# Matmul with rotary embedding on one core: two more block pairs, and stores in paced quarters

## The chip, the core and the metric

The kernel runs on one core of a Trainium2 chip. The metric is the device time of the program in microseconds (us). Before the change the median of three runs is 149.89 us (149.50 to 150.14). The execution that was profiled took 149.84 us, of which 148.1 us is the span from the first to the last instruction.

## The reference

```python
# x (16, 512, 768), weight (768, 768), cos and sin (512, 64), all float32; n_heads = 12
y = np.matmul(x, weight).reshape(16, 512, 12, 64)
y1, y2 = y[..., :32], y[..., 32:]
out1 = y1 * cos1 - y2 * sin1      # cos1, sin1: first 32 columns, one row per position
out2 = y2 * cos2 + y1 * sin2      # cos2, sin2: last 32 columns
out = np.concatenate([out1, out2], axis=-1).reshape(16, 512, 768)
```

25.2 MB of x come in and 25.2 MB go out; between them are one matrix product with a fixed 768x768 weight and a rotation that needs two products and a sum per element.

## The kernel before

**Tiles and groups.** The 8192 rows of x are cut into 64 tiles of 128 rows. Partition p of a tile holds position 4p + r of one batch, so a tile has one r and one batch. Four tiles with one r are a group (`QB = 4`), there are 16 groups (`LAST = 15`), and a group's second half, its third and fourth tile, is "pair (g, 1)".

**Two ways in.** An ordinary tile is loaded whole by SyncE (`load`, 128 rows of 3072 B, into one of `NX = 10` buffers xs), cast to fp16 on ScalarE (`cast`, xc<-xs), transposed on TensorE in twelve 64-row pieces (`turn_rows`, L272, into PSUM tile pt) and copied back by ScalarE (xt<-pt). A pair named in `BLOCKS` comes in as a block pair: four quarter loads (`load_quarter`, L226, each into 32 partitions, 256 pieces of 768 B), then one 32x32 block transpose on VectorE (`turn_pair`, L300) in place of TensorE's work. A block pair marked "sp" is loaded by SyncE into one of `NB = 3` buffers xb and cast by one wide ScalarE cast (`cast_pair`, xd<-xb). One marked "pool" is loaded by GpSimd, with the cast in the DMA, into xh. Before the change the block pairs are the second halves of groups 4 to 13 and 15; of these 5, 7, 9, 11, 13 and 15 are "sp".

**The product.** `walk` and `one` (L362) issue the matmuls of a pair as two interleaved streams of 64-row halves into six PSUM banks, three for each pair. When the banks of a unit are complete, `rope` has VectorE multiply them by cos and by the signed sin (L443) into a buffer tq, or into the memory of the raw weight w_raw, which is one of the three homes used in turn. GpSimd adds the two products into the output buffer ov (L465). There are `NOV = 4` output buffers, one for each group in turn, so the add of group g + 4 waits until the stores of group g have landed. The last three groups use smaller units, and the last one also sums some of its units on VectorE and TensorE. `ident32`, an fp32 identity for a TensorE sum in the very last group, lies in the memory of w_raw and is written by GpSimd in the iteration of tile 8 (L718); VectorE's next product in that home waits for it.

**What sets the order.** All is written out by hand in one loop over the tiles i. Iteration i issues, in this order: the matmuls of tile i with one `turns` among them, `rope` as units become complete, `bturns` (block transposes about four tiles ahead), another `turns`, `casts` (about six tiles ahead), `pool_loads` (twenty tiles ahead), and the stores listed under i in the table `stores`. Each engine works through its own instructions in that order; `Flow.do` puts semaphore waits where data demand it, and `Flow.settle` leaves out waits that are already implied. SyncE's loads follow the list `fetch`; `pump` issues from it as far as free buffers allow, and the quarters of an "sp" pair are mixed with the tile loads that come before its turn.

**Stores.** Groups 0 to 12 are stored from ScalarE's queue, half a group at a time (two tiles, 768 KB, 256 pieces of 3072 B; L497). Groups 13 and 14 are stored by SyncE, and the last group by both in smaller pieces. A store waits for the GpSimd adds of its half. For groups 4 to 9 the two halves stand under tiles 4g + 10 and 4g + 12.

Of the kernel before, what the change touches and what calls it, by code (L numbers as in the profile page):

```python
# [10 lines left out]
FP32 = mybir.dt.float32  # L11
# [5 lines left out]
class Flow:  # L17
# [24 lines left out]
    def do(self, e, make, reads=(), writes=(), dma=None, tick=True, after=0):  # L42
        need = {}
        for k in reads:
            for s, v in self.wrote.get(k, {}).items():
                need[s] = max(need.get(s, 0), v)
        for k in writes:
            for d in (self.wrote, self.readby):
                for s, v in d.get(k, {}).items():
                    need[s] = max(need.get(s, 0), v)  # L50
        if e == "pe":
            need.pop("pe", None)
            if after:
                need["pe"] = after
        waits = self.settle(e, need)
        for s, v in waits[:-1]:
            self.eng[e].wait_ge(self.sem(s), v)  # L57
        i = make(self.eng[e])
        if waits:
            s, v = waits[-1]  # L60
            i.wait_op(self.sem(s), v, "sem-ge")
        name, step = (dma, 16) if dma else (e, 1)
        self.sem(name)
        self.order[name] = len(self.order) + sum(self.count.values())
        at = self.count[name] + step
        if tick or dma:
            i.then_inc(self.sems[name], step)
            self.count[name] = at
            self.known[name, at] = dict(self.seen[e])
        for k in reads:  # L70
            d = self.readby.setdefault(k, {})
            d[name] = max(d.get(name, 0), at)
        for k in writes:
            self.wrote[k] = {name: at}
            self.readby[k] = {}
        return i
# [32 lines left out]
def kernel(  # L109
# [10 lines left out]
    nc = tc.nc  # L120
    f = Flow(nc, tc)
    do = f.do
    P = nc.NUM_PARTITIONS

    B, S, H = x.shape
# [6 lines left out]
    SB = S // P  # L132
    QB = 4
# [3 lines left out]
    LAST = NG - 1  # L137


    BLOCKS = {}  # L140
    for g in range(5, 14):
        BLOCKS[g, 1] = "pool" if g % 2 == 0 and g >= 4 else "sp"
    BLOCKS[LAST, 1] = "sp"
    BLOCKS[4, 1] = "pool"

    def sbuf(name, shape, dt):
        return nc.alloc_sbuf_tensor(name, shape, dt).ap()
# [3 lines left out]
    ident = sbuf("ident", [P, P], FP16)  # L151
# [13 lines left out]
    w_flat = w_raw.rearrange("p t e n -> p (t e n)")  # L165
# [7 lines left out]
        v = mem[:, base : base + 2 * n].rearrange("p (j n) -> p j n", j=2)  # L173
        return v[:, :, lo:hi], sorted(keys)

    ident32 = w_flat[:, 3072 : 3072 + P]
    HOMES0, HOMES, HOMESL = (0, 1024, 3072, 4096), (6144, 0, 3072), (0, 1024, 2048, 3072, 4096, 5120)
    ov_b = [sbuf(f"ov{i}", [P, QB * H], FP32) for i in range(NOV)]
    py = nc.alloc_psum_tensor("py", [P, 6 * 512], FP32).ap()
# [14 lines left out]
    def where(i):  # L194
        g, s = divmod(i, QB)
        return QB * (g // SB) + s, g % SB

    def pair_of(i):
        return i // QB, (i % QB) // 2
# [31 lines left out]
    def load_w(c, e="sp"):  # L231
        t, h = c
        do(e, lambda eng: eng.dma_start(out=w_raw[:, t, h], in_=wv[t, h]),  # L233
           writes=[f"wr{t}{h}"], dma=f"ov{t}_0" if h else f"xb{t}")

    def cast_w(c, e):
        t, h = c
# [249 lines left out]
    def store(g, c0, c1, e):  # L487
# [11 lines left out]
           dma=f"xs{c0 // 256 % NX}" if (c1 - c0) % H else f"ov{o}_{c0}")  # L499


    do("dve", lambda eng: eng.memset(cold, 0.0), writes=["cold"])  # L502
    do("pool", lambda eng: eng.memset(ident, 0.0), writes=["ident"])
    do("pool", lambda eng: eng.affine_select(
        out=ident, in_=ident, compare_op=mybir.AluOpType.not_equal, fill=1.0,
        base=0, pattern=[[-1, P]], channel_multiplier=1), writes=["ident"])

    order = [0, 1, "w0", 2, "w1", "w2", 3, "w3", "w4", "w5"]
    for k in order:
# [8 lines left out]


    fetch, quarters = [], []  # L520
    soon = [p for p in sorted(BLOCKS) if BLOCKS[p] == "sp"]
    for i in range(QB, NTILE):
        if soon and i >= max(2, soon[0][0] - 1) * QB:
            quarters += [(soon[0], q) for q in (0, 2, 1, 3)]
            soon.pop(0)
        if not is_block(i):
            fetch.append(i)
            for _ in range(2 if i == QB * (LAST - 1) else 1):
                if quarters:
                    fetch.append(quarters.pop(0))  # L530
        elif quarters and quarters[0][0] == pair_of(i):
            fetch.append(quarters.pop(0))
    fetched = [0]
# [110 lines left out]
    def pool_loads(upto):  # L644
        while state["pool"] < len(pool_pairs):
            gh = pool_pairs[state["pool"]]
            if gh[0] * QB + 2 * gh[1] >= upto:
                return
            for q in (0, 2, 1, 3):
                load_quarter(gh, q)  # L650
            state["pool"] += 1

    stores = {}
    for g in range(LAST):
        for h in (0, 2):
            i = QB * (g + 1) + h
            q = (g, h * H, (h + 2) * H, "act")
            if g < 3:
                i += g + 1
            elif g < LAST - 4:  # L660
                i += QB + (1 if g in (3, LAST - 5) else 2)
            elif g < LAST - 2:
                i = QB * (LAST - 2) + 2 * (g - LAST + 4) + h // 2
            else:
                q = q[:3] + ("sp",)
            stores.setdefault(i, []).append(q)

    C_AHEAD, T_AHEAD, B_AHEAD, P_AHEAD = 5, 3, 4, 20
    ROWS = QB * LAST - 2
# [18 lines left out]
    for i in range(QB, NTILE):  # L688
        g, s = divmod(i, QB)
        us = units(g)  # L690
        done_to = (s + 1) * H
        rows_on[0] = QB <= i <= QB * LAST
        if i == QB * (LAST - 2) + 2:
            cast_pair((LAST, 1))
            xb_used[0] += 1
        if i < ROWS:
            if s % 2 == 0:
                for r in range(2):
                    lines[r].extend(walk(i // 2, r))
            for n in range(1, 4):  # L700
                both((i - QB) * 4608 + n * 1536)
                if n == (1 if i > QB else 2):
                    turns(i + T_AHEAD, 1)
        if i == ROWS:
            both(NTILE * 4608)
        for n, p in enumerate(pieces(g, s)) if i >= ROWS else ():
            a, z, _, bank = p
            if n == 1 and i < QB * LAST:
                turns(i + T_AHEAD, 1)
            for c in CHUNKS:  # L710
                mm_piece(i, p, c, c == CHUNKS[0], c == CHUNKS[-1],
                         tick=c == CHUNKS[-1])
            for u in us:
                if u[1] == z:
                    rope(g, u)
        bturns(i + (B_AHEAD if i < QB * (LAST - 2) else 9))
        if i == 2 * QB:
            do("pool", lambda eng: eng.tensor_copy(out=ident32, in_=ident),  # L718
               reads=["ident"], writes=["ident32", "wr20"])
        turns(i + 1 + (T_AHEAD if i > QB else 2), 1)  # L720
        casts(i + 1 + (C_AHEAD if i > QB else 4), 1 + i % 2)
        pool_loads(i + P_AHEAD)
        for q in stores.get(i, ()):
            store(*q)
        if g == LAST:
            if s == 2:
                store(g, 0, H, "sp")
            if s == 3:
                store(g, H, 2 * H, "act")
# [44 lines left out]
```

## Time and profile before

| | before |
|---|---|
| median of 3 runs | 149.89 us (149.50 to 150.14) |
| the profiled execution | 149.84 us, span 148.1 us |
| TensorE matmul busy | 140.8 us |
| VectorE busy | 126.8 us |
| GpSimd busy | 123.3 us |
| ScalarE busy | 75.9 us |
| bytes moved by DMA | 51.27 MB |
| granted TensorE clock | 1.000 |

Times on the profile are counted from the first instruction. An engine's busy time is the union of its instructions; idle time in front of an instruction is put down to whatever ended it. In the chain of waits the program is followed backwards from its last instruction, so what does not stand in it had something else to hide behind. The DMA share is the time of all packets over that of 16 DMA engines; since packets overlap a little, a share of 1.03 is a full engine, and with several queues at work it reads up to 1.2.

### The profile page before, as it was taken

To read this page: it belongs to the slowest core of one execution; us is meant where nothing else is said; L and a number is where in the kernel's file an instruction comes from. 1 tells how busy PE (TensorE), PEld (TensorE's weight loads), DVE (VectorE), ACT (ScalarE), POOL (GpSimd) and SP (SyncE) were. 2 spreads that over 40 slices of the span, in tenths; PEclk is the share of its full clock that TensorE was granted. 3 is DMA by queue.
4 is the path that set the end of the run, shared out by engine and by line. 5 is a ranking of instruction groups with operands and counts; after the bars stand their busy time and mean duration, and the time that the engine had idled before them with its cause. 6 is when DMAs were issued, how large, how long until landed. Compare 5 with 4: busy or idle time off the path is not lost.

```text
span 148.1 us, 4361 instructions
## 1 busy us (share of the span) xinstructions
PE 140.8 (95%) x1918; PEld 112.8 (76%) x1918; DVE 126.8 (86%) x102; ACT 75.9 (51%) x90; POOL 123.3 (83%) x76
## 2 busy tenths in 40 slices
PE   6879999999999999999999999999999999999980
PEld 2335578888888888888888888888888888765860
DVE  0244999884999999899999998999989999999990
ACT  3444798787761933557261915375263919931010
POOL 1000399999999999999999999869899999899980
PEclk9999999999999999999999999999999999999999
DMA  4999999999999999999999999999999999998684
GB/s 125 344 394 400 401 401 400 303 351 319 332 351 343 319 336 290 328 408 296 326 362 394 375 310 360 347 400 328 371 380 360 411 412 415 414 402 320 238 309 172
DMA packets 28355, 51.27 MB, mean 346 GB/s; under 512 B 7216, under 2 KB 14128, under 8 KB 28336
## 3 DMA queue, kind: packets, MB, share of 16 engines
q1 hardware_dynamic: 15536, 28.05, 55.2%
q10 hardware_dynamic: 7360, 20.97, 36.0%
q0 software_dynamic: 5440, 1.97, 10.7%
q8 instruction: 15, 0.25, 0.7%
q14 instruction: 4, 0.03, 0.1%
HBM read 27.79 MB, written 25.17 MB: 358 GB/s over the span
## 4 chain that ended last, share of the span: by engine, by line
PE 78%; DVE 12%; DMA 5%; issue 2%; SPq 1%; DVEq 0%
PE py L362 68%; DVE tq L443 8%; PE py L337 5%; DMA w_raw<-in_weight_dram 5%; PE pt L272 4%; DVE w_raw L443 2%; SPq L211 1%; PE pt L257 1%; SPq L233 1%; DVE ov L412 1%; DVE py L405 0%; DVE xs L405 0%; DVE w_sb L191 0%; DVEq L57 0%; SPq L769 0%
## 5 line engine op out<-in xcount | busy, mean ns | idle before, releaser
L465 POOL TENSOR_TENSOR ov<-tq 128x512 f32<-128x512 f32 (+3 forms) x34 | 76.1, 2261 | 19.5 <-DVE tq L443 19.4
L362 PE MATMUL py<-w_sb,xt 64*128 64x512 f16 (+1 forms) x816 | 77.7, 323 | 0.0
L443 DVE TENSOR_TENSOR tq<-py,csn 128x1024 f32<-128x1024 f32 (+2 forms) x51 | 74.3, 1495 | 3.2 <-PE py L362 2.8
L362 PEld LDWEIGHTS py<-w_sb,xt 64*128 64x128 f16 x816 | 57.2, 94 | 10.3 <-DVE tq L443 0.4
L191 ACT COPY xt<-pt 128x768 f16<-128x768 f16 x40 | 32.0, 801 | 50.2 <-PE pt L272 49.0
L362 PE MATMUL py<-w_sb,xp 64*128 64x512 f16 (+1 forms) x480 | 47.5, 323 | 0.0
L191 ACT CAST xc<-xs 128x768 f16<-128x768 f32 x42 | 36.8, 909 | 7.2 <-DMA xs<-in_x_dram 7.1
L443 DVE TENSOR_TENSOR w_raw<-py,csn 128x1024 f32<-128x1024 f32 (+1 forms) x22 | 35.3, 1606 | 4.5 <-POOL w_raw L718 2.1
L362 PEld LDWEIGHTS py<-w_sb,xp 64*128 64x128 f16 x480 | 34.2, 94 | 5.5
L465 POOL TENSOR_TENSOR ov<-w_raw 128x1536 f32<-128x1536 f32 (+2 forms) x15 | 35.4, 2375 | 0.7 <-DVE w_raw L443 0.5
L337 PE MATMUL py<-w_sb,xt 128*128 128x256 f16 (+1 forms) x102 | 17.0, 317 | 1.5 <-DVE w_sb L191 1.3
L272 PEld LDWEIGHTS pt<-ident,xc 64*128 64x128 f16 x432 | 14.1, 95 | 1.3 <-issue 0.2
L337 PEld LDWEIGHTS py<-w_sb,xt 128*128 128x128 f16 x102 | 9.2, 98 | 7.5 <-DVE w_sb L191 2.8
L272 PE MATMUL pt<-ident,xc 64*128 64x64 f16 x432 | 14.1, 190 | 0.0
L226 POOL DMA_DIRECT2D xh<-in_x_dram x20 | 11.7, 590 | 0.0
L191 ACT CAST xd<-xb 128x1536 f16<-128x1536 f32 x6 | 9.8, 1641 | 0.0
L191 DVE CAST w_sb<-w_raw 128x768 f16<-128x768 f32 x6 | 3.4, 558 | 3.8 <-DMA w_raw<-in_weight_dram 3.8
L300 DVE STREAM_TRANSPOSE xp<-xh 128x768 f32<-128x768 f32 x5 | 6.2, 1236 | 0.0
L560 PE MATMUL py<-cold 128*128 128x512 f16 x12 | 4.8, 566 | 1.4 <-DVE cold L502 1.4
L300 DVE STREAM_TRANSPOSE xp<-xd 128x768 f32<-128x768 f32 x6 | 5.8, 970 | 0.0
L191 ACT COPY ov<-py 128x256 f32<-128x256 f32 x1 | 0.4, 373 | 10.0 <-PE py L475 10.0
L191 DVE COPY xt<-pt 128x768 f16<-128x768 f16 x2 | 1.1, 558 | 5.0 <-PE pt L257 5.0
(26 smaller groups left out, 23.0 us busy)
## 6 DMA issues: line engine op xcount, KB each, us to landing
out_dram<-ov ACTq DMA_DIRECT2D x26, 768.0 KB, 9.2
xs<-in_x_dram SPq DMA_DIRECT2D x42, 384.0 KB, 16.0
xb<-in_x_dram SPq DMA_DIRECT2D x24, 192.0 KB, 16.7
out_dram<-ov SPq DMA_DIRECT2D x4, 768.0 KB, 5.3
w_raw<-in_weight_dram SPq DMA_DIRECT2D x6, 384.0 KB, 7.1
xh<-in_x_dram POOLq DMA_DIRECT2D x20, 96.0 KB, 12.9
out_dram<-ov SPq DMA_DIRECT2D x1, 384.0 KB, 2.3
out_dram<-ov ACTq DMA_DIRECT2D x1, 384.0 KB, 2.4
```

The lines of the kernel that those rows point to most:

```text
L191: eng.copy(out=o, in_=i_) if e == "act" else eng.tensor_copy(out=o, in_=i_)
L211: do(e, lambda eng: eng.dma_start(out=xs_b[k], in_=x[b].rearrange("(p r) h -> r p h", r=SB)[r]), writes=[f"xs{k}"], dma=f"xs{k}")
L226: do(e, lambda eng: eng.dma_start(out=dst[ts(q, R)], in_=src[r, q]), writes=[f"{name}q{q}"], dma=name)
L233: do(e, lambda eng: eng.dma_start(out=w_raw[:, t, h], in_=wv[t, h]), writes=[f"wr{t}{h}"], dma=f"ov{t}_0" if h else f"xb{t}")
L257: do("pe", lambda eng: eng.transpose(pt[:, t, h, :], src[:, t, h, :], ident), reads=[f"xc{c}", "ident"], writes=[f"pt{k}"], tick=(t, h) == ...
L272: do("pe", lambda eng: eng.transpose(pts[r][:, t, h, :], src[rows, t, h, :], ident[rows, rows]), reads=[f"xc{c}", "ident"], writes=[f"pt{r ...
L300: do("dve", lambda eng: eng.transpose(out=dst, in_=src), reads=rd, writes=[f"xp{z}"])
L337: do("pe", lambda eng: eng.matmul(ps, get(t, h), w_sb[:, t, h, a - s * H : z - s * H], start=start, stop=stop), reads=[key, f"w{t}{h}"], w ...
L362: do("pe", lambda eng: eng.matmul(py[:, a:z], get(t, h)[rows], w_sb[rows, t, h, a - s * H : z - s * H], start=start, stop=not opens and en ...
L443: do("dve", lambda eng: eng.tensor_tensor(out=tq.rearrange("p j (h d) -> p j h d", d=D), in0=ps.rearrange("p (h d) -> p h d", d=D) .unsque ...
L465: do(adder, lambda eng: eng.tensor_tensor(out=ov_b[o][:, ds(c0, w)].rearrange("p (h t d) -> p h t d", t=2, d=HD), in0=tq[:, 0].rearrange(" ...
L560: do("pe", lambda eng: eng.matmul(py[:, ts(b, 512)], cold[:, 0:P], cold, start=True, stop=warmed[0] < WARM - 6), reads=["cold"], writes=[f ...
```

## The change

Pairs (2, 1) and (3, 1), that is tiles 10, 11, 14 and 15, become block pairs loaded by SyncE. Their quarters are not mixed among earlier tiles: they stand in `fetch` where the tile loads stood, quarters 0 and 2 in place of the first tile and 1 and 3 in place of the second. `ident32` gets memory of its own and is written at the start. The raw weight's loads use other semaphores. The stores of groups 0 to 12 are cut into quarters: two tiles by half of the columns (384 KB in 256 pieces of 1536 B). Quarter n = 4g + 2·(half of the tiles) + (half of the columns) of groups 0 to 10 stands under tile 5 + n + min(3, n // 5), which for groups 4 to 10 is one quarter under each of tiles 4g + 8 to 4g + 11; groups 11 and 12 have two quarters under each of tiles 52 to 55. A quarter also waits until TensorE has finished all it was given up to that point of the program.

```diff
     BLOCKS[4, 1] = "pool"
+    EARLY = ((2, 1), (3, 1))
+    for p in EARLY:
+        BLOCKS[p] = "sp"
...
-    ident32 = w_flat[:, 3072 : 3072 + P]
+    ident32 = sbuf("ident32", [P, P], FP32)
...
-           writes=[f"wr{t}{h}"], dma=f"ov{t}_0" if h else f"xb{t}")
+           writes=[f"wr{t}{h}"], dma=f"ov{t}_{1536 * (1 - h)}")
...
+    def store_half(g, h, c, at):
+
+        o = ov_of[g]
+        b, r = where(g * QB)
+        W = H // 2
+        dst = out.rearrange("b (p r) h -> r p b h", r=SB)[r, :, b + h : b + h + 2, ds(c * W, W)]
+        src = ov_b[o].rearrange("p (b h) -> p b h", b=QB)[:, h : h + 2, ds(c * W, W)]
+        for s, v in f.settle("act", {"pe": at}):
+            nc.scalar.wait_ge(f.sem(s), v)
+        do("act", lambda eng: eng.dma_start(out=dst, in_=src),
+           reads=[f"ov{o}c{z}" for s in (h, h + 1)
+                  for z in range(s * H + c * W, s * H + (c + 1) * W, 64)],
+           dma=f"ov{o}_{h * H}" + "ab"[c])
...
+    do("pool", lambda eng: eng.tensor_copy(out=ident32, in_=ident),
+       reads=["ident"], writes=["ident32"])
...
-    soon = [p for p in sorted(BLOCKS) if BLOCKS[p] == "sp"]
+    soon = [p for p in sorted(BLOCKS) if BLOCKS[p] == "sp" and p not in EARLY]
...
+        elif pair_of(i) in EARLY:
+            fetch += [(pair_of(i), q) for q in ((0, 2), (1, 3))[i % 2]]
...
-    stores = {}
-    for g in range(LAST):
+    stores, halves = {}, {}
+    for n in range(4 * (LAST - 2)):
+        g, (h, c) = n // 4, divmod(n % 4, 2)
+        i = 5 + n + min(3, n // 5) if g < LAST - 4 else QB * (LAST - 2) + (n - 4 * (LAST - 4)) // 2
+        halves.setdefault(i, []).append((g, 2 * h, c))
+    for g in range(LAST - 2, LAST):
         for h in (0, 2):
-            i = QB * (g + 1) + h
-            q = (g, h * H, (h + 2) * H, "act")
-            if g < 3:
-                i += g + 1
-            elif g < LAST - 4:
-                i += QB + (1 if g in (3, LAST - 5) else 2)
-            elif g < LAST - 2:
-                i = QB * (LAST - 2) + 2 * (g - LAST + 4) + h // 2
-            else:
-                q = q[:3] + ("sp",)
-            stores.setdefault(i, []).append(q)
+            stores.setdefault(QB * (g + 1) + h, []).append((g, h * H, (h + 2) * H, "sp"))
...
-        if i == 2 * QB:
-            do("pool", lambda eng: eng.tensor_copy(out=ident32, in_=ident),
-               reads=["ident"], writes=["ident32", "wr20"])
...
+        for q in halves.get(i, ()):
+            store_half(*q, f.count["pe"])
```

## The prediction

> **What bounds the kernel now.** I read the page's busy shares and chain first, then the chain in order of time, then VectorE's timeline, the waits and the DMA records.
>
> ```profile
> PE 140.8 (95%) x1918; PEld 112.8 (76%) x1918; DVE 126.8 (86%) x102; ACT 75.9 (51%) x90; POOL 123.3 (83%) x76
> DMA  4999999999999999999999999999999999998684
> PE 78%; DVE 12%; DMA 5%; issue 2%; SPq 1%; DVEq 0%
> ```
>
> TensorE holds 78% of the chain, but VectorE and GpSimd are over 80% busy, and the DMA engines are full until about 130 us. The chain in order of time shows what one tile's turn (L272) costs TensorE.
>
> ```profile
> 25.11 0.21 PE pt L272 x11
> 25.32 1.95 PE py L362 x18
> ...
> 33.62 0.20 PE pt L272 x11
> ...
> 48.17 0.17 PE pt L272 x10
> ...
> 56.32 0.17 PE pt L272 x10
> ...
> 125.76 0.03 issue
> 125.78 0.02 DVEq L57
> 125.81 0.04 issue
> 125.84 3.45 DVE tq L443 x3
> ```
>
> Four tiles with four turns take 33.62 - 25.11 = 8.51 us; four tiles with two turns and a block pair take 56.32 - 48.17 = 8.15 us. TensorE is on the chain without a break from 18.4 to 125.8 us; then VectorE is, up to the last stores. When VectorE last waited for TensorE is in its timeline:
>
> ```profile
> 108.73 1.23 DVE L443 TENSOR_TENSOR w_raw<-py,csn 128x1024 f32<-128x1024 f32 x1 [0.54 <-PE py L362]
> 116.89 2.36 DVE L443 TENSOR_TENSOR tq<-py,csn 128x1024 f32<-128x1024 f32 x2 [0.27 <-PE py L362]
> ```
>
> From 116.89 on it has hardly a gap. So VectorE's end moves as TensorE's work before 117 us moves, one for one, until something else is late.
>
> **The turns taken from TensorE.** Tiles 10, 11, 14 and 15 are turned between about 22 and 38 us, inside the unbroken stretch. Two turns are worth 8.51 - 8.15 = 0.36 us, four 0.72 us. Their matmuls stay, with xp in place of xt (323 ns mean in both rows): nothing. Term: -0.72 us.
>
> **VectorE** gains two block transposes:
>
> ```profile
> L300 DVE STREAM_TRANSPOSE xp<-xd 128x768 f32<-128x768 f32 x6 | 5.8, 970 | 0.0
> DVE w_raw L443 <- POOL w_raw L718: 2.1, 1, 2.1
> ```
>
> 2 x 0.97 = 1.94 us more between 27 and 37 us. In that stretch it idles 0.2 to 0.5 us before nearly every product, waiting for TensorE, and the wait of 2.1 us for `ident32` at 36.6 us goes, since that copy (0.30 us) moves to about 1.5 us, where GpSimd waits 15 us for its first add. TensorE did not stall behind the 2.1 us, so removing it gains nothing, and a VectorE lag of that size does no harm. Term: 0. Without this cover the 1.94 us would come back at VectorE's next gaps (0.54 us at 59.8, 0.28 at 68.0, 0.29 at 76.1), well before 117 us.
>
> **ScalarE** loses four casts of 909 ns and four copies of 801 ns and gains two wide casts of 1640 ns: 3.6 us less work. It gains 26 issues (0.38 us each, which run beside its copies in the timeline) and the wait for TensorE at a tile's end. Queued behind such a wait are the next casts and the next xt copy. A cast is made six tiles ahead and turned three or four ahead, so it may come two tiles (3.9 us) late before TensorE sees it; the wait holds it one tile at most. ScalarE idles some 3.5 us before one copy of each group anyway (L191 from L272: 49.0 us in 26 waits). Term: 0; if the cover were gone, up to one tile, 1.95 us, once.
>
> **GpSimd** waits for two store semaphores instead of one before 24 adds. No row has the price of a passed semaphore wait; the "issue" pieces of the chain are 0.02 to 0.06 us, so 0.5 to 1.4 us spread over 90 us. It has a gap of 1.88 us at 97.5. Term: 0, at most +1.
>
> **SyncE's queue.** Eight quarter loads replace four tile loads; everything from tile 12 on is queued behind them. In the trace's packet records a 3072 B packet takes 121 ns, a 768 B one 36 ns with its own queue alone and 49 ns beside GpSimd's loads. Over 16 engines: 4 x 128 x 121 = 62 us·engine go, 8 x 256 x 36 to 49 = 74 to 100 come: +0.7 to +2.4 us of full DMA. There is a worse row: where quarters flow without stores, the rate falls.
>
> ```profile
> 18.00:24.00 6.00, 6.00 (x96) 4.34 (x95) 5.47 (x5) 5.48 (x9) 5.24 (x3) 1.00 1.03 401
> 26.00:29.00 3.00, 3.00 (x49) 2.57 (x47) 2.34 (x3) 2.66 (x4) 2.98 (x3) 1.00 1.06 278
> 102.00:105.00 3.00, 3.00 (x41) 2.58 (x38) 3.00 (x3) 0.00 (x0) 2.39 (x1) 1.00 1.05 281
> 134.00:139.00 5.00, 5.00 (x38) 3.47 (x36) 4.88 (x6) 0.00 (x0) 5.00 (x5) 1.00 0.61 242
> 139.00:143.00 4.00, 4.00 (x39) 3.59 (x37) 4.00 (x9) 0.00 (x0) 4.00 (x4) 1.00 0.78 305
> ```
>
> (Columns: stretch, length, busy time of five engines, clock, DMA share, GB/s.) At 278 instead of 401 GB/s the two pairs' 1.57 MB would take 1.7 us longer, so loads from tile 16 on may land 1 to 4 us later. Setting each landing beside the cast that uses it, tile 16 lands 7.2 us early and tile 21 2.3 us; a late cast there has the two tiles of cover above. The tightest is the GpSimd-loaded pair (4, 1), landed 0.56 us before VectorE transposes it at 44.68, which is on another queue. Term: 0, upper bound +2.
>
> **The stores** are twice the packets at half the size. No row has 1536 B. Packets of 768, 1024, 2048 and 3072 B took 36, 47, 87 and 121 ns; between its neighbours 1536 B is 64 to 68 ns, so two cost 7 to 15 ns more than one of 3072. Times 6656 packets over 16 engines: +2.9 to +6.2 us of DMA. With the loads, +3.6 to +8.6 us, in a DMA system that is full until 130 us. What can hold it: the idle share from 134 us on, 0.39 x 5 + 0.22 x 4 + about 0.8 = 3.6 us, and the slow stretches ahead of a store's start, as at 26 and 102 us (3 us at 0.7 of the rate, 0.9 us each), some of which should go when stores flow all the time. I take 64 ns, the straight line through 768 and 3072, which fits the other two rows within 4 ns, and expect the extra work to end in the tail's room. Term: 0; bounds 0 and +5.
>
> A rule of the Trainium skill speaks against this change: "DMA: Bandwidth & Descriptors", section Bandwidth, asks for DMAs of 1 MiB or more, and gives about 2.0 us fixed per DMA; by that, 26 more DMAs one after another would be an estimated +52 us. The trace does not agree that fixed times add up here: with several DMAs under way the share stays at 1.03 or above.
>
> **Sum.** 149.84 - 0.72 = 149.12 us, 0.77 below the median of the three runs.
>
> **Rivals.**
>
> *ScalarE's queue fills (slower).* When all three queues have work, each gets as many packets as the others: from 96 to 100 us the records have 339 packets on SyncE's and 356 on ScalarE's. With GpSimd's queue too (46 to 50 us: 331 on SyncE's, 255 on ScalarE's, 331 on GpSimd's) a round over 16 engines takes 193 ns, of which the store has 0.77 x 121 = 93. With 65 for the store it is 165, or 97 store packets per us, where quarters need 1024 per 8.15 us = 126. GpSimd's loads run for some 50 us, so 1450 packets, 5.7 quarters, pile up on top of the 4 or 5 that a landing time of 9 us means. SyncE's own issue shows the limit: at 57.68 us, with 2048 pieces (8 quarters) outstanding, it is held for 5.2 us. If ScalarE is held like that, a quarter takes 2.64 us instead of 2.04, and casts and copies stand behind it. It decides once ScalarE is over 4 us late: two groups at 0.6 us per quarter use that up, and the burst of eight quarters at tiles 52 to 55 adds to it. I price it at 2.2 us net of the gain: 151.3. Against it: SyncE's queue empties when it runs into its own buffers, and GpSimd's loads end near 97 us. By the Trainium skill, same page, section Queues, rings and completion order, each engine goes round the queues packet by packet; on that the trace's counts agree.
>
> *The tail pays (about the same).* The extra DMA work overflows the 3.6 us by 0.5 to 1, or late stores of groups 10 and 11 hold GpSimd's last adds (gaps there: 0.45 and 0.34 us): 149.7 to 150.1, say 149.9. For it: the upper price.
>
> *Starved.* The early quarters put tiles 16 to 25 4 us behind and TensorE waits 2 us: 151.1. Against it: the slack above.
>
> **How the numbers follow.** Forecast 0.50, full queue 0.25, tail 0.17, starved 0.08. A measurement here tells 0.5% (0.75 us) from nothing, so "faster" is below 149.14 and "slower" above 150.64. The forecast sits on that line: three quarters of its chance go to faster, since a turn may also free a little time around it, the rest to same. Faster 0.38; same 0.12 + 0.14 = 0.26; slower 0.25 + 0.08 + 0.03 = 0.36. Range 148.6 (a turn worth 0.3) to 151.8 (either slow case half a microsecond dearer); the forecast's own is 148.6 to 149.6.
>
> **What would show it.** L272 falls to 384 matmuls; periods of four tiles between 22 and 40 us are near 8.15; the chain stays on TensorE to about 125.0. No ScalarE wait for DMA past 20 us, no GpSimd wait for a store. The stores' DMA issues by ScalarE stay near 0.4 us each; several of 1 us or more mean the full queue. The tail's DMA share rises and its length stays. I am wrong if TensorE has idle time between 40 and 117 us, or if the span from its end to the last landing grows.

## The result, and the profile after

Timed in turns with the kernel before, the changed kernel took 151.59 us (median of 4, 150.60 to 152.65) against 150.01: ratio 1.0116, 95% interval 1.0067 to 1.0165. Timed again later, it took 150.88 (median of 12, 149.66 to 152.15) against 149.95: ratio 1.0044 (1.0019 to 1.0069). It is slower, by 0.4 to 1.2%, and not, as forecast, faster; the time lies inside the predicted range. Ratios leave out executions that the chip disturbed, so one can lie nearer to 1 than the two medians beside it.

The profiled execution took 151.3 us (span 149.5). Its line numbers are the changed kernel's (L275 is L272 before, L365 is L362, L514 issues the quarter stores). From its page: busy times, DMA share and GB/s in 40 slices, and the chain by engine.

```profile
PE 140.7 (94%) x1870; PEld 110.9 (74%) x1870; DVE 128.3 (86%) x104; ACT 74.9 (50%) x84; POOL 123.3 (82%) x76
...
DMA  4999999999999999999999999999999999999784
GB/s 127 356 397 398 402 273 291 243 261 331 329 331 327 332 331 326 349 383 328 326 350 401 342 330 327 392 401 389 397 390 406 396 399 393 399 407 373 300 319 162
...
PE 62%; DVE 13%; DMA 8%; SPq 8%; issue 3%; ACTq 2%; ACT 1%; DVEq 0%
```

The engines do about the same work as before. New in the chain are 8% DMA, 8% SyncE issue and 2% ScalarE issue. The DMA row reads full while slices 6 to 9 (19 to 34 us) move 243 to 291 GB/s: full time, few bytes. The same in stretches (stretch, length, busy times of five engines, clock, DMA share, GB/s); the first three lines are the kernel before, the last three the changed one:

```profile
20.00:24.00 4.00, 4.00 (x82) 3.54 (x79) 3.47 (x3) 3.48 (x6) 4.00 (x3) 1.00 1.03 400
24.00:28.00 4.00, 4.00 (x74) 3.42 (x71) 3.34 (x3) 3.66 (x6) 3.98 (x6) 1.00 1.06 319
28.00:35.00 7.00, 7.00 (x119) 6.01 (x117) 5.76 (x3) 5.44 (x8) 6.99 (x6) 1.00 1.09 360
...
20.00:24.00 4.00, 4.00 (x76) 3.47 (x71) 3.48 (x3) 3.48 (x6) 4.00 (x3) 1.00 1.08 257
24.00:28.00 4.00, 3.69 (x57) 2.84 (x52) 3.53 (x3) 2.98 (x4) 3.99 (x6) 1.00 1.09 257
28.00:35.00 7.00, 6.84 (x103) 5.83 (x105) 6.15 (x4) 4.61 (x6) 6.99 (x6) 1.00 1.14 273
```

What follows from it is in the chain in order of time (start, length, what):

```profile
13.22 12.47 DMA xb<-in_x_dram
26.20 0.46 ACTq L514
26.66 0.53 issue
27.19 0.83 ACT xt L194
28.16 3.46 PE py L365 x31
...
82.97 3.17 PE py L365 x28
86.19 2.15 DVE w_raw L446
88.35 2.64 ACTq L514
91.03 0.81 ACT xt L194
92.23 5.85 PE py L365 x56
...
127.19 3.44 DVE tq L446 x3
```

Before, the chain is on TensorE without a break from 18.4 to 125.8 us. Now it comes out of a load: the quarters of pair (2, 1) issued at 13.22 us, landed at 25.69. ScalarE's cast waits for them, then the first stores and an xt copy stand behind it. At 88 us it goes through a ScalarE store issue that is held for 2.64 us. ScalarE's timeline at both places (start, length, line, work; in brackets idle time before it and what ended it):

```profile
25.71 1.60 ACT L194 CAST xd<-xb 128x1536 f16<-128x1536 f32 x1 [1.02 <-DMA xb<-in_x_dram]
25.72 0.95 ACTq L514 DMA_DIRECT2D out_dram<-ov  x2
27.19 0.82 ACT L194 COPY xt<-pt 128x768 f16<-128x768 f16 x1
...
70.67 1.01 ACTq L514 DMA_DIRECT2D out_dram<-ov  x1
...
83.39 2.48 ACTq L514 DMA_DIRECT2D out_dram<-ov  x1
...
88.30 2.69 ACTq L514 DMA_DIRECT2D out_dram<-ov  x1
91.03 0.80 ACT L194 COPY xt<-pt 128x768 f16<-128x768 f16 x1 [1.89 <-PE py L365]
```

The reader sees a cast that starts 0.02 us after its data, for which ScalarE had waited 1.02 us, and issues that grow from 1 us at 70 us to 2.7 at 88 (before: 0.35 to 0.51 throughout); the copy at 91.03 starts when the held issue is over, not when TensorE (named as releaser, that is, as what ended the wait) was done. TensorE's idle time after 20 us is 0.46 us before 28.16, 0.94 before 91.88 and 0.22 before 127.01, each ended by an xt copy. From the waits (total, times, longest), the kernel before first:

```profile
ACT xc L191 <- DMA xs<-in_x_dram: 7.1, 5, 2.4
ACT xt L191 <- PE pt L272: 49.0, 26, 3.6
...
ACT xc L194 <- DMA xs<-in_x_dram: 19.6, 10, 3.0
ACT xt L194 <- PE pt L275: 17.9, 17, 2.3
```

ScalarE went from waiting for TensorE to waiting for loads.

**A measure used below.** Single executions already differ by up to 1.7 us at 21 us, mostly by when the raw weight lands. So each trace is laid beside that of before, product matmul by product matmul (the four turns are not product matmuls): how late it is (us) at number 72 of those recorded, counted from 0 (21 us), at number 144 (27.5), 288 (40) and 828 (86), and at VectorE's last product (144 us). The difference of last and first column is what the kernel itself won or lost.

```
                 72nd   144th   288th   828th    last   last - 72nd
stores_only     +0.32   +0.32   +0.32   +0.32   +0.31   -0.01
only_31         -0.14   -0.14   -0.49   -0.49   -0.48   -0.34
plain_load      +0.52   +0.35   -0.18   -0.18   -0.18   -0.70
spread_pieces   -0.87   -1.04   -1.57   -1.57   -1.56   -0.69
plain_halves    -0.49   -0.66   -1.19   -1.18   -0.36   +0.13
only_21         -0.06   +1.03   +0.86   +0.82   +0.85   +0.91
after           -0.19   -0.36   -0.13   -0.16   +1.35   +1.54
after_again     +0.04   +0.78   +0.26   +0.22   +0.40   +0.36
after_rounds    +0.30   +1.62   +1.09   +1.06   +1.73   +1.43
cast_later      +0.06   +0.89   +0.36   +0.32   +0.41   +0.35
code_earlier    -0.13   +0.79   +2.69   +2.65   +2.69   +2.82
```

### The profile page after: what moved, and what is told of

It reads as the page before. It is cut to its first block, busy times and chain, and to the rows that moved or that the text cites. A ratio compares the mean times of both kernels' runs of the same rounds, so it can differ in the third digit from the quotient of the medians.

```text
span 149.5 us, 4306 instructions
## 1 busy us (share of the span) xinstructions
PE 140.7 (94%) x1870; PEld 110.9 (74%) x1870; DVE 128.3 (86%) x104; ACT 74.9 (50%) x84; POOL 123.3 (82%) x76
## 4 chain that ended last, share of the span: by engine, by line
PE 62%; DVE 13%; DMA 8%; SPq 8%; issue 3%; ACTq 2%; ACT 1%; DVEq 0%
PE py L365 59%; DMA xb<-in_x_dram 8%; DVE tq L446 7%; DVE w_raw L446 4%; PE pt L275 3%; SPq L214 3%; ACTq L514 2%; SPq L236 2%; SPq L229 2%; ACT xt L194 1%; DVE ov L415 1%; DVE py L408 0%; DVE xs L408 0%; SPq L534 0%; SPq L536 0%
## 5 line engine op out<-in xcount | busy, mean ns | idle before, releaser
L365 PE MATMUL py<-w_sb,xt 64*128 64x256 f16 (+1 forms) x720 | 70.5, 323 | 0.5 <-ACT xt L194 0.5
L365 PEld LDWEIGHTS py<-w_sb,xt 64*128 64x128 f16 x720 | 50.9, 94 | 10.6 <-DVE tq L446 1.2
L365 PE MATMUL py<-w_sb,xp 64*128 64x256 f16 (+1 forms) x576 | 57.0, 323 | 0.0
L194 ACT CAST xc<-xs 128x768 f16<-128x768 f32 x38 | 34.3, 907 | 31.7 <-DMA xs<-in_x_dram 19.6
L365 PEld LDWEIGHTS py<-w_sb,xp 64*128 64x128 f16 x576 | 41.0, 94 | 6.8
L194 ACT COPY xt<-pt 128x768 f16<-128x768 f16 x36 | 28.7, 800 | 26.7 <-PE pt L275 17.9
L275 PEld LDWEIGHTS pt<-ident,xc 64*128 64x128 f16 x384 | 12.3, 95 | 3.0 <-ACT xt L194 1.8
L275 PE MATMUL pt<-ident,xc 64*128 64x64 f16 x384 | 12.7, 191 | 1.2 <-ACT xt L194 1.2
L194 ACT CAST xd<-xb 128x1536 f16<-128x1536 f32 x8 | 13.1, 1633 | 1.4 <-DMA xb<-in_x_dram 1.0
L303 DVE STREAM_TRANSPOSE xp<-xd 128x768 f32<-128x768 f32 x8 | 7.7, 969 | 0.3 <-ACT xd L194 0.3
```

What stands on the lines that cost most here:

```text
L194: eng.copy(out=o, in_=i_) if e == "act" else eng.tensor_copy(out=o, in_=i_)
L275: do("pe", lambda eng: eng.transpose(pts[r][:, t, h, :], src[rows, t, h, :], ident[rows, rows]), reads=[f"xc{c}", "ident"], writes=[f"pt{r ...
L303: do("dve", lambda eng: eng.transpose(out=dst, in_=src), reads=rd, writes=[f"xp{z}"])
L365: do("pe", lambda eng: eng.matmul(py[:, a:z], get(t, h)[rows], w_sb[rows, t, h, a - s * H : z - s * H], start=start, stop=not opens and en ...
```

## The experiments

Each diff is against the changed kernel unless said. Ratios are to the kernel before, timed in turns with it, with 95% intervals.

### The two halves of the change

**pairs_only**: the early pairs with the old half-group stores (the table of stores is that of before).

> The two early pairs and the moved identity stay; the stores are those of the kernel before (halves of 768 KB in pieces of 3072 B, no wait for TensorE). Theory A (ScalarE's DMA queue fills with pieces of 1536 B, and ScalarE is held at its issues): no issue by ScalarE over 0.6 us, TensorE without idle time after 40 us, time 149.3 to 150.0, i.e. 0.72 us for the turns less what the late early pair costs at 28 us (about 0.8). Theory B (the early pairs are the loss, through the loads they delay): 151 or more, ScalarE still waits for xs loads between 28 and 70 us.

156.05 us (median of 4, 153.11 to 156.94). There is no ratio. TensorE's granted clock is 0.92 in the mean from 126 to 147 us of the profiled execution, so times after 126 us are not compared. Its waits:

```profile
ACT xc L194 <- DMA xs<-in_x_dram: 30.4, 16, 3.3
ACT xt L194 <- PE pt L275: 29.8, 20, 3.9
```

No issue of ScalarE is held. TensorE idles 0.99 us before 27.25 and 3.18 us before 129.73, there for an xt copy behind late casts, and even the shortest run is above the four first times of the changed kernel. The held issues of the changed kernel are therefore not the root; without them the shortage shows as waits for loads.

**stores_only**: no early pairs, quarter stores.

```diff
-    EARLY = ((2, 1), (3, 1))
+    EARLY = ()
```

> No early pairs (tiles 10, 11, 14 and 15 are loaded and turned as before); the stores are the paced quarters. Theory A: ScalarE's issues grow to 1.3 to 2.7 us from about 70 us on, TensorE idles near 90 and 127 us, time 151.0 to 151.8, 1.0 to 1.8 over before. Theory B: within 0.3 of before.

149.91 us, 10 runs, ratio 1.0025 (0.9995 to 1.0056). Most issues from 93 us on are held, up to 2.3 us, TensorE never idles after 20 us, and the row of the table says -0.01 us. Half-sized stores and a filling queue cost nothing that shows by themselves.

**whole_rows**: 52 stores of one whole tile (128 pieces of 3072 B) in the places of the quarters, to take away the number of pieces.

```diff
-        dst = out.rearrange("b (p r) h -> r p b h", r=SB)[r, :, b + h : b + h + 2, ds(c * W, W)]
-        src = ov_b[o].rearrange("p (b h) -> p b h", b=QB)[:, h : h + 2, ds(c * W, W)]
+        dst = out.rearrange("b (p r) h -> r p b h", r=SB)[r, :, b + h + c, :]
+        src = ov_b[o].rearrange("p (b h) -> p b h", b=QB)[:, h + c, :]
```

> As the changed kernel, with the same number of stores at the same places, of the same bytes and with the same wait for TensorE, but each is one whole tile (128 pieces of 3072 B) in place of half the columns of two tiles (256 pieces of 1536 B). Theory A: at most 4 or 5 stores of 128 pieces outstanding, no held issue, time 149.4 to 150.2 (the stall at 28 us stays). If instead the number of DMA issues or the wait for TensorE is what costs (theory C), the time stays near 151.5 and ScalarE's casts are as late as in the changed kernel.

154.06 us (4 runs, 151.80 to 156.22, no ratio): no held issue before 131 us, and ScalarE waits 36.7 us for loads (17 times); TensorE idles six times, longest before 26.8, 84.4 and 129.6 us. As in pairs_only, taking the fill away does not help.

**no_pace**: the wait for TensorE before each store is left out.

```diff
-        for s, v in f.settle("act", {"pe": at}):
-            nc.scalar.wait_ge(f.sem(s), v)
```

> As the changed kernel, without the wait for TensorE in front of a quarter store; a store still waits for GpSimd's adds. Theory A: the queue fills all the same, 151 to 152. Theory C (the wait for TensorE makes ScalarE late): 149.3 to 150.0.

151.38 us (4 runs), ratio 1.0122 (1.0068 to 1.0176), as the changed kernel then was. The pacing isn't the cause.

### The early pairs

**plain_load**: the early pairs come by two loads of a whole tile each, as ordinary tiles do. The rows of tiles 10, 11, 14 and 15 then hold other values; all work after the loads is the same.

```diff
+        if gh in EARLY:
+            if q < 2:
+                do(e, lambda eng: eng.dma_start(
+                    out=buf[:, ts(q, H)], in_=x[b + q].rearrange("(p r) h -> r p h", r=SB)[r]),
+                   writes=[f"{name}q{q}", f"{name}q{q + 2}"], dma=name)
+            return
```

> As the changed kernel, but each early pair comes in as two whole-tile loads (128 pieces of 3072 B over all partitions) into the same buffer, at the same place in SyncE's list; the same bytes, casts, transposes and matmuls run, only the rows of tiles 10, 11, 14 and 15 hold other values than the reference's. Theory D (the quarter loads, with nothing of another queue beside them between 20 and 35 us, lose some 2.8 us of DMA time that the full DMA never gets back): GB/s between 20 and 27 us back to about 400, no wait of TensorE at 28 us, time 149.0 to 149.6. Theory A' (what costs is ScalarE's queue filling with the quarter stores once the pairs are there): ScalarE held near 90 us as before, time 150.5 or more.

149.50 us, 10 runs, ratio 0.9951 (0.9918 to 0.9983), no TensorE idle after 20 us, -0.70 us in the table. Its stretches, the first of them 261 GB/s in the changed kernel:

```profile
20.00:27.00 7.00, 7.00 (x127) 5.84 (x125) 6.05 (x4) 6.48 (x9) 7.00 (x6) 1.00 1.05 384
27.00:35.00 8.00, 8.00 (x122) 6.89 (x119) 7.61 (x5) 5.27 (x7) 7.97 (x8) 1.00 1.10 323
```

ScalarE's store issues are held here too, up to 2.05 us at 99 us, and TensorE does not notice. With other loads the forecast comes true. All of the loss is in how the early pairs are loaded.

**only_31** and **only_21**: one early pair each (`EARLY = ((3, 1),)` and `((2, 1),)`).

> Only pair (3, 1) is an early block pair; tiles 10 and 11 are ordinary tiles again. The stores stay as changed. Theory D: its quarters come after the first stores and GpSimd loads have begun or nearly so, so half or less of the loss: DMA time lost between 20 and 35 us about 2.3 us in place of 3.9 (before 1.1), turns worth 0.36 us, time 149.5 to 150.3. If the two pairs cost in proportion to their number only: 150.6 to 150.9.

> Only pair (2, 1) is an early block pair. Theory D: its quarters flow alone right after 20 us, so this pair has the larger part of the loss (2.5 to 3 us lost between 20 and 35 us) and the stall at 28 us: time 150.2 to 151.2, not below only_31.

only_31: 150.48 us, 10 runs, ratio 1.0023 (0.9980 to 1.0066), no idle, -0.34 us in the table: two turns, as reckoned, though the ten times together do not show the gain. only_21: 150.97, ratio 1.0071 (1.0032 to 1.0110), TensorE idle 0.95 us before 27.05. The pair loaded first, before the first store, does the harm.

**spread_pieces**: as plain_load (the same tiles with other values), but in pieces of 768 B, four in each of 128 partitions, to part the size of a piece from the number of partitions it goes to.

```diff
+                do(e, lambda eng: eng.dma_start(
+                    out=buf.rearrange("p (j t k) -> p j t k", t=2, j=NQ)[:, :, q, :],
+                    in_=x[b + q].rearrange("(p r) (j k) -> r p j k", r=SB, j=NQ)[r]),
```

> As plain_load, but each of the two whole-tile loads of an early pair is cut into pieces of 768 B over all 128 partitions (512 pieces, so the same number and size of pieces as the pair's four quarters, which go to 32 partitions each); the rows of tiles 10, 11, 14 and 15 hold other values than the reference's. Theory P (a quarter's 32 partitions take less than the full rate when nothing else flows beside it): the rate between 20 and 27 us is 360 GB/s or more (384 with plain loads, 261 in the changed kernel), time 149.0 to 149.8. Theory S (768 B pieces themselves are slow in a row): 261 to 300 GB/s there and 150.8 to 151.8.

149.24 us, 10 runs, ratio 0.9952 (0.9915 to 0.9988), 358 GB/s from 20 to 27 us:

```profile
20.00:27.00 7.00, 7.00 (x120) 5.97 (x117) 6.01 (x5) 6.49 (x9) 6.98 (x8) 1.00 1.07 358
```

In the packet records a 768 B packet takes 56 to 60 ns in the mean where quarters flow alone (20.0 to 22.3 and 25.2 to 28.0 us of the changed kernel), 39 to 40 here. So small pieces are not the trouble. What is left is that a quarter lands in only 32 partitions, or that it gathers its pieces from many rows of x, while this run takes the four pieces of a row together. The packets of wide_pairs below are gathered as the quarters' are but land in 128 partitions, and they took 36 ns each (21 to 25 us). That speaks for the 32 partitions, though at a quarter of the rate.

The Trainium skill has a rule for this that the prediction missed: "SBUF — State Buffer", section "Door 1: The DMA port swizzle (why `[64,N]` ≈ `[32,N]`)", says that a transfer into partitions 0 to 31 reaches 8 of 16 ports, and gives 189 GB/s at 1 MiB. From 19.9 to 21.2 us of the changed kernel's profile only quarters and one instruction packet flow, at 242 GB/s: below the full rate, as the rule has it, but above its figure. Ports are not told apart in these records.

**plain_halves**: plain_load (the same other values) with the old half stores.

> As plain_load (whole-tile loads for the early pairs, other values in tiles 10, 11, 14 and 15), with the stores of the kernel before: halves of 768 KB, no wait for TensorE. If the store quarters neither gain nor cost once the loads are not behind: 149.0 to 149.7, the same as plain_load, and no held issue on ScalarE. If the quarters' share of the DMA engines is needed for the gain: 150 or more and ScalarE waiting for loads after 60 us.

150.55 us (10 runs, 148.55 to 154.18), ratio 0.9935 (0.9905 to 0.9966): by the ratio no different from plain_load. The gain can be had without the quarter stores. The profiled execution, though, gave its gain back at the end: before 125.30 us TensorE idled 0.69 us for an xt copy that stood behind a wide cast. ScalarE had waited 3.45 us for GpSimd before 120.59 and 0.73 us for the load of that cast. Neither profile with other loads and quarter stores (plain_load, spread_pieces) shows such a stall.

**early_by_pool**: GpSimd loads the early pairs, cast in the DMA, behind ScalarE's fourth cast.

```diff
-        BLOCKS[p] = "sp"
+        BLOCKS[p] = "pool"
...
+    for s, v in f.settle("pool", {"act": f.count["act"]}):
+        nc.gpsimd.wait_ge(f.sem(s), v)
+    for gh in EARLY:
+        for q in (0, 2, 1, 3):
+            load_quarter(gh, q)
```

> The two early pairs are loaded by GpSimd (with the cast in the DMA) as soon as ScalarE has made its fourth cast, about 12 us, beside SyncE's tile loads, in place of SyncE's quarters; everything else as changed. Theory D: quarters that run beside another queue's traffic lose little: DMA time lost between 20 and 35 us below 2, no stall at 28 us, time 149.0 to 149.8. If the stores are what costs (A'): 150.5 or more. A risk of its own: tiles 6 to 9, with 1.1 to 2.9 us of slack, are delayed and TensorE waits for them.

153.29 us (4 runs), ratio 1.0214 (1.0137 to 1.0291). It trades one wait for another: VectorE waits for GpSimd's pairs (idle time in brackets).

```profile
38.28 1.23 DVE L303 STREAM_TRANSPOSE xp<-xh 128x768 f32<-128x768 f32 x1 [2.01 <-DMA xh<-in_x_dram]
...
48.85 1.23 DVE L303 STREAM_TRANSPOSE xp<-xh 128x768 f32<-128x768 f32 x1 [2.70 <-DMA xh<-in_x_dram]
```

**two_queues**: quarters 2 and 3 of the early pairs go from ScalarE's queue.

```diff
-            fetch += [(pair_of(i), q) for q in ((0, 2), (1, 3))[i % 2]]
+            fetch.append((pair_of(i), i % 2))
...
+    for q in (2, 3):
+        load_quarter((2, 1), q, "act")
...
+    for q in (2, 3):
+        load_quarter((3, 1), q, "act")
```

> The changed kernel with all results as the reference's; of each early pair SyncE loads quarters 0 and 1 at their place and ScalarE issues quarters 2 and 3 from its own, still empty queue, after its casts of tiles 5 and 7. Theory P: quarters that flow from two queues write to both halves of the partitions in turn, so the rate between 20 and 27 us is 340 GB/s or more, no stall of TensorE near 28 us, time 149.2 to 149.9. If the quarters are slow whatever their queue: 260 to 300 GB/s and 150.8 to 151.8.

152.31 us (4 runs), ratio 1.0156 (1.0079 to 1.0233), 278 GB/s, pair (2, 1) landed at 27.93. ScalarE's packets began only at 20.5 us, so it is a poor test of quarters side by side, but it is no way out.

**wide_pairs** and **wide_all**: the right values in all 128 partitions, by eight loads for each pair, one for each 32-row block; in wide_all for all eight SyncE pairs (the condition is `e == "sp"`).

```diff
+        if gh in EARLY:
+            for j in (2 * q, 2 * q + 1):
+                do(e, lambda eng: eng.dma_start(out=dst[:, j], in_=src[r, :, :, j]),
+                   writes=[f"{name}q{j}"], dma=name)
+            return
...
-           reads=[f"xb{k}q{q}" for q in range(NQ)], writes=[f"xd{c}"])
+           reads=[f"xb{k}q{q}" for q in range(2 * NQ)], writes=[f"xd{c}"])
```

> Right values, and the early pairs land on all partitions: eight loads for each pair, one for each 32-row block of its two tiles, into all 128 partitions in 128 pieces of 768 B, where the changed kernel has four loads into 32 partitions each. Theory P (what costs is that a quarter ends in only 32 partitions): 355 GB/s or more in 20 to 27 us, pair (2,1) lands before 24 us, no TensorE idle at 27 to 28 us, no store issue over 2 us before 95 us, 149.2 to 149.6 us, ratio to before under 1.000. Rival (768 B pieces from scattered rows, or the number of DMAs, cost by themselves): 300 GB/s or less in 20 to 27 us, TensorE idle at 27 to 28 us, 150.8 us or more.

> As wide_pairs, and the six other SyncE pairs, of groups 5, 7, 9, 11, 13 and 15, come in the same way. If narrow loads cost wherever they flow: the full-rate time lost from 35 to 126 us falls by 1 us or more and loads have more slack, 148.6 to 149.2 us. If narrow loads are hidden wherever stores flow beside them: as wide_pairs within 0.3 us. If more DMA issues on SyncE hurt: slower than wide_pairs by over 0.3 us.

169.34 us (ratio 1.1265, 1.1204 to 1.1326) and 201.91 (1.3423, 1.3361 to 1.3486). Both theories missed it. SyncE's own timeline in wide_pairs:

```profile
9.58 1.03 SPq L214 DMA_DIRECT2D xs<-in_x_dram  x2
10.65 12.61 SPq L231 DMA_DIRECT2D xb<-in_x_dram  x8
```

And the DMA and GB/s rows of its page, in slices of 4.2 us:

```profile
DMA  4999739993399999999999999999999977995685
GB/s 139 374 409 401 285 98 254 273 252 82 79 256 236 306 401 374 360 320 330 395 367 329 328 385 362 331 327 391 395 403 398 376 272 278 362 364 206 236 325 184
```

Eight issues take 12.6 us, and where these loads flow the rate is 79 to 98 GB/s, a quarter of 400. The Trainium skill, "DMA: Bandwidth & Descriptors", section "Why a DMA increments its semaphore by 16 and not by 1", says that a DMA uses the largest number of engines up to 16 that divides the outermost size of both access patterns; here the source's is 4. A quarter of the rate agrees with 4 engines of 16, and so does the DMA row, which reads 3 tenths in those slices; engines are not told apart in these records. So the time of this run does not speak on narrow loads, and it remains untried whether the right values can be spread over 128 partitions at full rate.

### The stall at 27 us, and where it goes

**cast_later**: the wide cast of pair (2, 1) moves one iteration back, behind an xt copy and a store issue.

```diff
+            elif i == 10:
+                pass
...
+        if i == 6:
+            cast_pair((2, 1))
+            xb_used[0] += 1
```

> The changed kernel with all its loads and stores; ScalarE makes the cast of pair (2, 1) one iteration later, behind the copy of the next transposed tile that in the changed kernel stood behind it. If the loss is a sum of separate stalls (the late pair at 28 us, the held issues at 91 and 127 us): no idle time of TensorE at 28 us, the rest as it was, so 150.7 to 151.0. If the full DMA sets the total and a stall only shows where it is paid: TensorE runs ahead by 0.5 to 0.8 us after 30 us and gives it back at the held issues of ScalarE, 151.3 to 151.8.

150.31 us, 12 runs, ratio 1.0018 (0.9987 to 1.0049), better than either expectation. It looked like a repair. But the profile still had TensorE idle 0.68 us before 26.90, so the changed kernel was profiled again (**after_again**), and then both were timed on one chip (**after_rounds**, **cast_later_2**).

> The changed kernel once more, for one question: is TensorE's idle at 27 us, which six variants show after a 16 KB packet of the instruction queue, tied to that packet? Theory I (TensorE waits for its instructions): if the packet that is read between 19 and 27 us ends after 25 us, TensorE has an idle of 0.5 to 1.2 us that ends 1.2 to 1.6 us after the packet and is put down to nothing; if it ends before 24.5 us, there is no such idle. Rival (the idle is a wait that the profile does not name): no such relation. Time 150.6 to 152.6 us.

> The changed kernel again, timed beside before, with one more profile. Theory S (the early pairs make one stall near 27 us, worth about what the turns save, and in some executions a second one, of ScalarE's store issues): 150.2 to 150.6 us where only the first occurs, 151.3 to 152.6 where the second does, ratio to before 1.003 to 1.012. Rival (it is slower by the same amount in every execution): all within 0.5 us, ratio 1.010 to 1.013.

> cast_later again, on the same chip as after_rounds. If moving that one cast really removes a loss, its median is 0.5 us or more below that of after_rounds; if cast_later only looked better because the two were timed in different jobs, the two medians agree within 0.3 us.

after_again took 150.35 us, after_rounds 150.88 (ratio 1.0044, above) and cast_later_2 151.08 (1.0045, 1.0019 to 1.0071). On one chip the two kernels are the same; cast_later is no repair. What made its first ratio better (another chip, at another time) is not shown. The changed kernel's executions are not alike: 1.54, 0.36 and 1.43 us lost by the table. In after_again the stall at 27 us has no releaser and no later one follows:

```profile
25.36 0.84 PE py L365 x7
26.20 0.59 issue
26.80 5.18 PE py L365 x47
```

What ends it was sought among the DMA packets. TensorE's idle is put down to nothing in nine profiles of the early pair (2, 1), and each has a 16 KB packet of an instruction queue that ends late:

```
                packet ends   idle ends   between
no_pace            26.83        28.09       1.26
two_queues         25.34        26.69       1.35
whole_rows         25.41        26.77       1.36
after_again        25.39        26.80       1.41
pairs_only         25.80        27.25       1.45
cast_later_2       26.19        27.66       1.47
only_21            25.54        27.05       1.51
cast_later         25.35        26.90       1.55
after_rounds       25.90        27.63       1.73
no such idle: packet ends 21.12 (before), 21.15 (after), 23.26 (spread_pieces),
23.59 (only_31), 24.01 (stores_only), 24.08 (early_by_pool), 24.20 (plain_load),
22.48 (plain_halves)
```

In after_again the view of DMA queues from 24.3 to 25.4 us (packets, MB, share of 16 engines) shows it among SyncE's packets:

```profile
q1 hardware_dynamic: 254, 0.38, 96.6%
q8 instruction: 1, 0.02, 6.2%
```

**code_earlier** puts 56 small instructions ahead on TensorE, in its waiting time at the start, so that the next 16 KB are wanted earlier.

```diff
+            W = P if warmed[0] < WARM - 6 else 512
+            for z in range(0, 512, W):
...
+    for _ in range(20):
+        nc.tensor.wait_ge(f.sem("dve"), 1)
```

> The changed kernel with 56 more small instructions on TensorE before its first real matmul (six warm-up matmuls cut in four, and 20 waits that are already satisfied, where TensorE waits for the weight), so that the place where its next 16 KB of instructions is needed comes some 1.6 us earlier, before the slow stretch of the early quarters. Theory I (the idle at 27 us is TensorE waiting for its instructions): the first 16 KB packet ends before 24 us, the idle that is put down to nothing goes or is under 0.3 us, and TensorE's matmul number 144 stands at -0.2 to +0.3 us against before, set against number 72; 149.3 to 150.2 us, ratio under 1.002, unless ScalarE's stall at 28 us or its held issues take over. Rival (something else holds TensorE there): the idle stays at 26.1 to 28 us with 0.6 us or more whatever the packet does, ratio 1.004 or more.

The packet ended at 18.25 us and the idle without a releaser was gone, as theory I said. But the time was 152.56 (ratio 1.0189, 1.0139 to 1.0239), not the 149.3 to 150.2 named for it: now the loads were late. Tile 8 landed at 22.16 (19.57 in after_again), pair (2, 1) at 27.43 (24.23 in after_again), and ScalarE waited:

```profile
20.19 0.91 ACT L194 CAST xc<-xs 128x768 f16<-128x768 f32 x1 [0.59 <-DMA xs<-in_x_dram]
...
22.18 0.90 ACT L194 CAST xc<-xs 128x768 f16<-128x768 f32 x1 [0.39 <-DMA xs<-in_x_dram]
...
27.45 1.61 ACT L194 CAST xd<-xb 128x1536 f16<-128x1536 f32 x1 [1.60 <-DMA xb<-in_x_dram]
```

In this profile TensorE idles four times behind xt copies between 21 and 40 us, the longest 0.99 us before 29.91. That TensorE waits at 27 us for its own instructions is thus supported by ten profiles, the last of them a direct test. That the packet, read early, is what made the loads late (its reading takes 1.1 us, and the changed kernel's first profile, with the packet at 19.96, has its pair late too) is only argued. So is what makes it late: in no profile without SyncE's quarters of pair (2, 1) did it end after 24.20 us, but in two with them it ended by 21.2.

## Why the prediction was wrong

- **The sum's one gain was right.** Four turns were put at -0.72 us: -0.70 in plain_load, -0.69 in spread_pieces, and -0.34 for two of them in only_31.
- **VectorE, GpSimd, the stores: 0, and nothing else shows.** stores_only, which has the stores and the moved `ident32`, is at -0.01 us; plain_load, which has all the rest too, loses nothing. The extra packets found room, as the prediction thought possible: with an estimated 7 ns plus 0.0363 ns per byte for each packet (a line through the records), the time from 35 to 126 us that packets do not fill falls by 3.8 us, from 8.9 before to 5.1 in the changed kernel. The estimated +52 us does not show either. The 2.0 us for it stand in the Trainium skill, "DMA: Bandwidth & Descriptors", under "Anatomy of one DMA — SWDGE (gpsimd) path", that is for DMAs issued by GpSimd, and not under Bandwidth.
- **The step that failed is "SyncE's queue", Term: 0.** Its own row was right: 278 GB/s where quarters flow alone; measured 243 to 291. Its lateness of 1 to 4 us was a little short: tile 12 landed 3.2 us later than before (27.45 against 24.23), tile 16 5.2 us (34.68 against 29.48). Wrong was that nothing waits for it. The slack was read for tiles 16 and 21, behind the pairs; tile 25's in the trace before, 1.24 us, was passed over. The pair itself, late by its own slowness, was not looked up: in the first profile it landed at 25.69, 1.0 us after ScalarE was free for its cast. ScalarE's queue is in order, so an xt copy stood behind that cast; the "two tiles of cover" hold for a late cast, not for the copy of another tile behind it. In after_again the pair landed at 24.23 and its cast waited for nothing; the stall there is that of the next point.
- **A wait was left out: TensorE's instructions** come by DMA too, in packets among those of the loads. No term had them. The stalls at 27 us cost about 0.9 us in after_again and 1.5 in after_rounds (144th less 72nd, plus the 0.17 us that plain_load has won by then), more than the turns had given.
- **The rival "ScalarE's queue fills"** had the sign, the time (151.3) and, in the first profile, the place: issues over 1 us from 70 us on, and 1.15 us lost at 91 us. But it is not the cause: stores_only fills the queue and loses nothing; pairs_only and whole_rows do not fill it and lose no less. It is one place where the shortage comes out.
- **The rival "Starved" had the cause, and a chance of 0.08.** It named the early quarters and 151.1 us. The evidence against it, "the slack above", was the failed step. Its path was only in part right: ScalarE did wait 2.7 to 3.0 us for later tiles (at 38.7, 46.8, 55.1 and 63.0 us of the first profile), but TensorE first stood still at 27 us, for the pair or for its instructions.
- **What would show it**: L275 has its 384 matmuls, as said. ScalarE's waits for DMA past 20 us, issues of several us, and TensorE's idle time between 40 and 117 us (0.94 us before 91.88) were to speak against the forecast; the first profile has all three.
- **"The tail pays"** is out: stores_only keeps its delay of 0.32 us to VectorE's last product, and in the changed kernel the delay stays at 1.3 us from 127 us on.

Open are three things: why the lateness of the loads is made up in some executions and ends in held issues of ScalarE in others; what makes an instruction packet late, and whether an early one delays loads; and a load with the right values that isn't narrow. No kernel with the right values beat the kernel before.

## What to carry to other kernels

Before a transfer is moved to another form, read its rate where it flows alone, and set its own landing beside its own first use, not only those behind it: the work saved (0.7 us) was won only where loads kept slack. A loss must be looked for where it starts; here a wait for loads, a held store issue and an idle without a releaser all turned up behind one slow stretch that begins at 20 us. And a variant timed in another job, or one profile, can show a repair that isn't one: time it beside the original, and subtract what was already late before the change.

## What the runs showed of the hardware

- From 20 to 24 us, where loads into 32 partitions flow among others, the rate was 224 to 257 GB/s (code_earlier, the changed kernel); with whole tiles into 128 partitions there it was 400 (before). With 768 B pieces spread over 128 partitions it was 358 from 20 to 27 us, where the changed kernel has 261.
- Where loads with an outermost size of 4 flowed, the rate was 79 to 98 GB/s, and their issues took 1.6 us for each 96 KB.
- Most of ScalarE's held issues began with 7 stores of 256 pieces outstanding (1792), and one of these had landed when the issue ended; SyncE had been held at 2048 (before, 57.68 us).
- TensorE's instructions come in 16 KB packets, each 0.9 to 1.4 us long; where the one between 19 and 27 us ended after 25 us, TensorE started again 1.26 to 1.73 us after its end.
